# An encoder kernel whose weight, sum and working tiles start 32 bytes later in SBUF

## The chip, the cores and the metric

The kernel runs on one core of one Trainium2 chip. The metric is the device time of one execution in microseconds; several executions are made and their median is compared. SBUF is the on-chip memory of the core, 128 partitions deep; an address below is the byte offset within a partition, the same for all 128.

## The reference

The computation is a two-layer encoder over 256 tokens of width 1024, in float32. Per layer:

```
x = x + 0.5 * swiglu(rms_norm(x, ffn1_norm[l]), ffn1_w_gate[l], ffn1_w_up[l], ffn1_w_down[l])
h = rms_norm(x, mix_norm[l])
proj = h @ w_in[l]
qa, ka, va, qb, kb, vb = jnp.split(proj, SPLITS, axis=-1)
out_a = windowed_gqa_sink(qa, ka, va, sink[l], slopes_a)
out_b = differential_attention(qb, kb, vb, lam, slopes_b)
out_b = (rms_norm(out_b, diff_subln[l]) * (1.0 - lam_init)).reshape(b, s, B_V_COLS)
x = x + jnp.concatenate([out_a, out_b], axis=-1) @ w_out[l]
x = x + 0.5 * swiglu(rms_norm(x, ffn2_norm[l]), ffn2_w_gate[l], ffn2_w_up[l], ffn2_w_down[l])
```

and `swiglu(h, w_gate, w_up, w_down)` is `(silu(h @ w_gate) * (h @ w_up)) @ w_down` with a hidden width of 2816. A last RMS norm gives the output. Nearly all of the arithmetic is in the matrix products with the weights: four feed-forward blocks and two attention blocks.

## The kernel before

Every product with a weight is made with three matmuls. A weight arrives in SBUF as float32 in a raw tile (`emit_dma`, line 164; tag `raw`, 6 buffers of 8192 bytes per partition). `emit_split` (line 207) turns a raw tile into a high and a low part: ScalarE casts to float32r (`hi`), VectorE subtracts (`lo = raw - hi`). The parts lie in the pool `s4` (28 buffers of 4096 bytes), which also holds the activations, split in the same way. `tokens` (line 613) then issues, for each chunk of 128 of the contraction and each of the two blocks of 128 tokens, `xh*hi`, `xl*hi` and `xh*lo` into one PSUM bank. The activation is the stationary operand (128 x 128) and the weight the moving one (128 x 512 columns, 2048 bytes of each partition).

Within a feed-forward block the hidden width is walked in groups of 512 columns. In most groups `by_sevens` (line 745) replaces the eight products of a 2 x 2 block form by seven products of sums: `prod` (line 709) issues them, with sums of weights made in the raw tiles (by VectorE, or by a transfer that adds while it writes) and sums of activations made once per block by `make_sums` in working tiles with the tags `q` and `v` (line 401). In the attention block `narrow` (line 637) has the weight as the stationary operand and the activation as the moving one, 512 columns wide for `hi` and 256 for `lo`; `scores` (line 989) multiplies queries and keys on half of the rows, two at a time; products of probabilities and values use plain float32. Transposes go through TensorE, with the data as stationary operand and `ident` as moving one.

The order of the matmuls is the program's own (`pe` keeps it always, line 69), and the other engines keep the program's order in the feed-forward blocks. How early a weight is fetched and split is set by `ahead` (line 248) with the tuned numbers in `LEAD` (line 32). A scheduler places the instructions of the attention block by a model of their times.

Memory: four pools lie one behind the other, and each tile takes a multiple of 32 bytes.

```
const = ctx.enter_context(tc.tile_pool(name="const", bufs=1))
wp = ctx.enter_context(tc.tile_pool(name="wp", bufs=1))
s4 = ctx.enter_context(tc.tile_pool(name="s4", bufs=N_S4))
tp = ctx.enter_context(tc.tile_pool(name="tp", bufs=1))
```

The pool `const` holds the residual stream `xk`, the identity `ident`, small constants and the tables of distances; `wp` the raw weights; `s4` split weights and activations; `tp` working tiles. In the kernel before, the tiles lie here:

| tile (pool) | first address | beyond a multiple of 64 |
|---|---|---|
| xk (const) | 16512 | 0 |
| ident (const) | 25216 | 0 |
| wake (const) | 25728 | 0 |
| ones (const) | 26272 | 32 |
| distB, distA (const) | 27552, 29600 | 32 |
| gsub, lex (const, the last two) | 32096, 32128 | 32, 0 |
| raw (wp), 6 of 8192 bytes | 32160 | 32 |
| s and w (s4), 28 of 4096 bytes | 81312 | 32 |
| tmp (tp), 5 of 2048 bytes | 198304 | 32 |
| q (tp), 3 of 4096 bytes | 208544 | 32 |
| v (tp), 4096 bytes | 220832 | 32 |
| vA (tp), 1024 bytes | 226336 | 32 |

In the profile the tiles of `s4` are named `w` (split weights) and `s` (all else), and almost all instructions have the line of the helper that records them, so groups are told apart by their tiles and shapes. A row of the timeline merges neighbours of one kind.

Of the kernel before, what the change touches and what calls it, by code (L numbers as in the profile page):

```python
# [9 lines left out]
F32 = mybir.dt.float32  # L10
# [4 lines left out]
P = 128  # L15
# [31 lines left out]
def trunk(ctx: ExitStack, tc: tile.TileContext, x, n1, g1, u1, d1, nm, w_in, sink,  # L47
# [23 lines left out]
    const = ctx.enter_context(tc.tile_pool(name="const", bufs=1))  # L71
# [479 lines left out]
    lsum = const.tile([P, 2, DEPTH], F32, name="lsum")  # L551
    nlam = const.tile([P, DEPTH], F32, name="nlam")
    gsub = const.tile([P, DEPTH], F32, name="gsub")
    slopeA = [2.0 ** -(h + 1) for h in range(8)]
    slopeB = [2.0 ** -(2 * (h + 1)) for h in range(4)]
    lam_init = [0.8 - 0.6 * math.exp(-0.3 * l) for l in range(DEPTH)]
# [733 lines left out]
```

## Time and profile before

| what | value |
|---|---|
| time, three runs | 909.51, 909.10, 909.54 us; median 909.51 us |
| span of the profiled execution, first to last instruction | 907.5 us |
| median less that span | 2.0 us |
| mean granted clock of TensorE | 0.999 |
| TensorE busy | 899.1 us |
| VectorE busy | 785.9 us |
| ScalarE busy | 609.8 us |
| read from HBM | 199.0 MB, 220 GB/s over the span |

For the profiled execution only its span is recorded, not a time of its own; the times come from separate executions. Engines are named PE (TensorE's matmuls), PEld (its weight loads), DVE (VectorE), ACT (ScalarE), POOL (GpSimd) and SP (a queue for transfers). A row of a group gives its tiles as out<-in, its shape, its count, then busy microseconds, the mean nanoseconds of one, and the idle time of the engine before it with what ended it. A matmul's busy span reaches over the start of the next one, so how fast matmuls follow each other is read from starts.

### The profile page before, as it was taken

How to read it: one execution, taken by the hardware profiler on the slowest of the kernel's cores; microseconds unless marked ns; L12 is line 12 of the kernel's file. 1: busy time of each engine (PE TensorE's matmuls, PEld its weight loads, DVE VectorE, ACT ScalarE, POOL GpSimd, SP SyncE). 2: the span in 40 equal slices, each digit the busy share in tenths (PEclk: the TensorE clock that was granted, in tenths of full speed). 3: DMA queues.
4: the chain of work that ended last, by engine and by line, in shares of the span. 5: the costliest groups of instructions: out<-in, count | busy, mean ns of one | idle time of the engine just before them, and what ended most of it. 6: DMA issues, size and time to landing. Idle time of an engine off the chain costs nothing.

```text
span 907.5 us, 12030 instructions
## 1 busy us (share of the span) xinstructions
PE 899.1 (99%) x4468; PEld 751.0 (83%) x4468; DVE 785.9 (87%) x1069; ACT 609.8 (67%) x970; POOL 63.2 (7%) x79
## 2 busy tenths in 40 slices
PE   9999999999999999999999999999999999999997
PEld 7888888888888888888888888888888888888886
DVE  5968999879987899999778999988888978999894
ACT  6946677666776776677575776667667785776660
POOL 0401000000001001000000001000000000101011
PEclk9999999999999999999999999999999999999999
DMA  9998897954148798897976898899611786898731
GB/s 328 355 287 213 236 309 247 268 143 179 47 150 241 174 265 247 247 300 256 279 204 171 250 278 258 252 303 248 182 57 48 263 223 166 234 312 255 219 114 47
DMA packets 114331, 200.83 MB, mean 221 GB/s; under 512 B 3678, under 2 KB 31648, under 8 KB 114272
## 3 DMA queue, kind: packets, MB, share of 16 engines
q1 hardware_dynamic: 97616, 167.66, 54.4%
q0 software_dynamic: 16096, 31.75, 20.1%
q8 instruction: 35, 0.57, 0.2%
q10 hardware_dynamic: 560, 0.66, 0.2%
q14 instruction: 24, 0.20, 0.1%
HBM read 199.00 MB, written 1.05 MB: 220 GB/s over the span
## 4 chain that ended last, share of the span: by engine, by line
PE 98%; DMA 1%; issue 0%; SPq 0%; DVE 0%; POOLq 0%; POOL 0%
PE ps L62 73%; PE xy L62 25%; DMA xk<-in_x_dram 1%; SPq L172 0%; DVE s L62 0%; DVE xk L62 0%; POOLq L1285 0%; POOL rf L62 0%; SPq L469 0%; SPq L465 0%; DVE tot L62 0%; DVE tmp L62 0%
## 5 line engine op out<-in xcount | busy, mean ns | idle before, releaser
L62 DVE TENSOR_TENSOR w<-raw,w 128x1024 fp32r<-128x1024 f32 (+1 forms) x458 | 476.4, 1097 | 34.6 <-ACT w L62 33.2
L62 PE MATMUL ps<-w,s 128*128 128x512 f32 (+1 forms) x2046 | 473.6, 389 | 0.0
L62 PEld LDWEIGHTS ps<-w,s 128*128 128x128 f32 x2046 | 379.9, 188 | 78.7 <-issue 0.8
L62 ACT CAST w<-raw 128x1024 fp32r<-128x1024 f32 (+1 forms) x457 | 403.9, 954 | 54.0 <-DVE raw L62 38.7
L62 PE MATMUL xy<-w,s 128*128 128x512 f32 x528 | 125.8, 392 | 0.0
L62 PEld LDWEIGHTS xy<-w,s 128*128 128x128 f32 x528 | 98.2, 188 | 20.4
L62 PE MATMUL xy<-w,q 128*128 128x512 f32 x360 | 88.1, 393 | 0.0
L62 PEld LDWEIGHTS xy<-w,q 128*128 128x128 f32 x360 | 66.5, 188 | 13.3
L62 PE MATMUL ps<-s,w 128*128 128x512 f32 (+1 forms) x384 | 69.8, 338 | 0.0
L62 DVE TENSOR_TENSOR raw<-raw,raw 128x2048 f32<-128x2048 f32 x30 | 68.6, 2288 | 0.5
L62 POOL DMA_DIRECT2D raw<-in_ffn_w_up_dram x30 | 38.9, 1313 | 430.1 <-DVE w L62 264.9
L62 PEld LDWEIGHTS ps<-s,w 128*128 128x128 f32 x384 | 58.6, 188 | 8.5
L62 ACT ACTIVATE s<-ps,gcol 128x256 fp32r<-128x256 f32 (+1 forms) x80 | 31.4, 479 | 34.0 <-PE ps L62 34.0
L62 ACT CAST s<-ps 128x512 fp32r<-128x512 f32 x36 | 20.4, 592 | 43.2 <-PE ps L62 43.0
L62 PE MATMUL ps<-w,q 128*128 128x512 f32 x180 | 43.2, 389 | 0.0
L62 PE MATMUL ps<-w,v 128*128 128x512 f32 x180 | 43.2, 389 | 0.0
L62 DVE TENSOR_TENSOR s<-ps,s 128x512 fp32r<-128x512 f32 x36 | 24.1, 686 | 19.5 <-ACT s L62 19.3
L62 PEld LDWEIGHTS ps<-w,v 128*128 128x128 f32 x180 | 33.8, 188 | 7.0
L62 PEld LDWEIGHTS ps<-w,q 128*128 128x128 f32 x180 | 33.8, 188 | 7.0
L62 ACT ACTIVATE s<-s,negm 128x256 f32<-128x256 f32 x64 | 31.8, 498 | 5.3 <-DVE negm L62 5.3
L62 ACT COPY ps<-ps 128x512 f32<-128x512 f32 x15 | 8.6, 570 | 34.4 <-PE ps L62 34.4
L62 DVE SCALAR_TENSOR_TENSOR s<-ps,gcol,s 128x256 fp32r<-128x256 f32 x48 | 20.3, 477 | 13.0 <-ACT s L62 12.9
(131 smaller groups left out, 584.3 us busy)
## 6 DMA issues: line engine op xcount, KB each, us to landing
raw<-in_ffn_w_down_dram SPq DMA_DIRECT2D x44, 1024.0 KB, 7.0
raw<-in_ffn_w_gate_dram SPq DMA_DIRECT2D x39, 1024.0 KB, 7.7
raw<-in_ffn_w_up_dram SPq DMA_DIRECT2D x39, 1024.0 KB, 7.1
raw<-in_ffn_w_up_dram POOLq DMA_DIRECT2D x30, 1024.0 KB, 10.0
raw<-in_w_in_dram SPq DMA_DIRECT2D x14, 1024.0 KB, 6.7
raw<-in_ffn_w_gate_dram SPq DMA_DIRECT2D x8, 512.0 KB, 7.9
raw<-in_ffn_w_up_dram SPq DMA_DIRECT2D x8, 512.0 KB, 8.9
raw<-in_w_in_dram SPq DMA_DIRECT2D x8, 512.0 KB, 6.0
```

The lines of the kernel that those rows point to most:

```text
L62: ins = issue(*a, **k)
```

## The change

One tile is added at the end of the list of constants. No instruction writes or reads it.

```
     lsum = const.tile([P, 2, DEPTH], F32, name="lsum")
     nlam = const.tile([P, DEPTH], F32, name="nlam")
     gsub = const.tile([P, DEPTH], F32, name="gsub")
+    const.tile([P, 8], F32, name="edge")
     slopeA = [2.0 ** -(h + 1) for h in range(8)]
```

It takes 8 floats, 32 bytes of each partition, between `gsub` and `lex`. All that lies behind it starts 32 bytes later: `lex`, and the pools `wp`, `s4` and `tp` as wholes. The raw tiles then start at 32192, the tiles of `s4` at 81344, `tmp` at 198336, `q` at 208576, `v` at 220864 and `vA` at 226368, all multiples of 64. What lies in front of it, `xk`, `ident`, `wake`, `ones` and the tables of distances among it, stays. The instructions are the same.

More of the change, by code (lines that the diff above doesn't have):

```diff
@@ L553, in trunk @@
     gsub = const.tile([P, DEPTH], F32, name="gsub")
+    const.tile([P, 8], F32, name="edge")
     slopeA = [2.0 ** -(h + 1) for h in range(8)]
```

## The prediction

> **What bounds the kernel now.** The page of the profile comes first: the span, the engines' busy shares and the chain of work that ended last.
>
> ```profile
> span 907.5 us, 12030 instructions
> PE 899.1 (99%) x4468; PEld 751.0 (83%) x4468; DVE 785.9 (87%) x1069; ACT 609.8 (67%) x970; POOL 63.2 (7%) x79
> ...
> PEclk9999999999999999999999999999999999999999
> ...
> PE 98%; DMA 1%; issue 0%; SPq 0%; DVE 0%; POOLq 0%; POOL 0%
> ```
>
> TensorE carries 98% of the chain at a full granted clock. The view of waits of TensorE has two rows in the whole run:
>
> ```profile
> PE ps L62 <- DVE wake L62: 1.0, 1, 1.0
> PE ps L62 <- DMA xk<-in_x_dram: 0.7, 1, 0.7
> ```
>
> Both lie in the first microseconds, so after the start no transfer and no other engine holds TensorE up. The time is then the sum of the intervals at which matmuls follow each other. Busy time can't give these, because one matmul's busy span (389 ns) overlaps the next; starts in the timeline of TensorE can. First a stretch in the middle, then two stretches of the end, whose first rows start in the same run of 256-column matmuls, then attention.
>
> ```profile
> 305.36 1.04 PE L62 MATMUL ps<-ident,s 128*128 128x128 f32 x8
> 306.19 3.01 PE L62 MATMUL xy<-w,q 128*128 128x512 f32 x12
> 309.04 8.32 PE L62 MATMUL ps<-w,s 128*128 128x512 f32 x36
> 317.20 2.88 PE L62 MATMUL ps<-w,q 128*128 128x512 f32 x12
> ```
>
> ```profile
> 896.82 4.00 PE L62 MATMUL ps<-w,s 128*128 128x256 f32 x32
> ...
> 898.74 2.08 PE L62 MATMUL ps<-w,s 128*128 128x256 f32 x16
> ```
>
> ```profile
> 244.63 2.78 PE L62 MATMUL ps<-ident,s 128*128 128x128 f32 x24
> 247.25 3.74 PE L62 MATMUL xy<-v,s 128*128 128x128 f32 x32
> 250.82 1.91 PE L62 MATMUL ps<-ident,s 128*128 128x128 f32 x16
> ```
>
> From the start of one row to the start of the next, divided by the count: 512 columns take 8.16 us / 36 = 226.7 ns; 256 columns take (898.74 - 896.82) / 16 = 120.0 ns. The difference of 106.7 ns for 256 columns is 0.417 ns a column, and what is left is a constant: 226.7 - 512 x 0.417 = 13.3 ns per matmul, the same at both widths. That constant is the one thing in the bound that an address could touch.
>
> **The change, part by part.** It adds a tile of 8 floats, 32 bytes per partition, that nothing reads or writes. It removes no instruction, adds no wait and moves nothing past a queue. All raw weights, split weights, sums and working tiles go from 32 past a multiple of 64 to a multiple of 64; xk, ident and wake, in front of the new tile, stay at multiples of 64, and ones stays at 32 past. Since all moved tiles go together, which of them lie beside each other is unchanged. Four kinds of access remain.
>
> VectorE, ScalarE and their operands: no cost. xk lies at a multiple of 64 already, tmp does not, and the same operation takes the same time:
>
> ```profile
> L62 DVE TENSOR_TENSOR tmp<-xy,tmp 128x512 f32<-128x512 f32 x30 | 19.2, 680 | 0.0
> ...
> L62 DVE TENSOR_TENSOR xk<-xk,ps 128x512 f32<-128x512 f32 x17 | 11.2, 681 | 2.2 <-PE ps L62 2.2
> ```
>
> Weight loads: no cost either. A transpose loads its data as weights, from s (32 past) or from xk (a multiple), 140 against 142 ns:
>
> ```profile
> L62 PEld LDWEIGHTS ps<-ident,s 128*128 128x128 f32 x240 | 28.0, 140 | 3.8
> L62 PEld LDWEIGHTS ps<-ident,xk 128*128 128x128 f32 x96 | 11.4, 142 | 2.9 <-DMA xk<-in_x_dram 1.1
> ```
>
> Transfers into raw: no row shows their price by address. It is covered as long as TensorE waits for none of them; without that cover the first stretch below would show it.
>
> Moving operands of matmuls: this is the open price. Every fast matmul streams w, s or q, now 32 past a multiple; no row has the same form with a moving operand at a multiple. The groups by form give the counts:
>
> ```profile
> L62 PE MATMUL ps<-w,s 128*128 128x512 f32 x2010 | 469.3, 390 | 0.0
> L62 PE MATMUL xy<-w,s 128*128 128x512 f32 x528 | 125.8, 392 | 0.0
> L62 PE MATMUL xy<-w,q 128*128 128x512 f32 x360 | 88.1, 393 | 0.0
> L62 PE MATMUL ps<-s,w 128*128 128x512 f32 x192 | 68.2, 398 | 0.0
> L62 PE MATMUL ps<-s,w 128*128 128x256 f32 x192 | 53.5, 278 | 0.0
> L62 PE MATMUL ps<-w,q 128*128 128x512 f32 x180 | 43.2, 389 | 0.0
> L62 PE MATMUL ps<-w,v 128*128 128x512 f32 x180 | 43.2, 389 | 0.0
> L62 PE MATMUL xy<-s,w 128*128 128x512 f32 x32 | 11.5, 395 | 0.0
> L62 PE MATMUL ps<-s,q 64*128 64x256 f32 x144 | 10.7, 289 | 0.0
> L62 PE MATMUL xy<-s,w 128*128 128x256 f32 x32 | 8.9, 278 | 0.0
> L62 PE MATMUL ps<-w,s 128*128 128x256 f32 x36 | 4.5, 283 | 0.0
> L62 PE MATMUL xy<-s,q 64*128 64x256 f32 x48 | 3.5, 279 | 0.0
> ```
>
> That is 3482 of 512 columns, 260 of 256, and 192 on half the rows that run in pairs and count as 96: 3838 in all. Each could gain between nothing and its whole constant, 13.3 ns: 0 to 51 us. Below nothing is the third rival. Between the ends there is one pair of rows that differs in the moving operand's address at one width, though also in the kind of work: transposes stream ident (a multiple) at 2.62 us / 24 = 109.2 ns, products stream v (32 past) at 3.57 us / 32 = 111.6 ns. They say 2.4 ns, or 9 us over 3838. My own value comes from counting: a run of 2048 bytes that starts 32 past a multiple of 64 touches 33 units of 64 bytes and not 32, a run of 1024 bytes 17 and not 16, so both widths pay one unit, as the constant does. A unit is 16 columns, 16 x 0.417 = 6.7 ns. It lies in the middle of the bounds, and I take it: 3838 x 6.7 = 25.6 us.
>
> [...]
>
> What is late next? The windows of single stages say it (length, then PE, PEld, DVE, ACT and POOL busy, clock, share of the DMA engines, GB/s):
>
> ```profile
> 19.60:69.40 49.80, 49.80 (x229) 41.20 (x228) 38.56 (x47) 35.07 (x52) 12.52 (x31) 1.00 1.04 324
> ...
> 401.60:432.40 30.80, 30.80 (x142) 25.60 (x141) 29.65 (x28) 22.25 (x26) 0.00 (x0) 1.00 0.81 269
> ...
> 515.60:546.40 30.80, 30.80 (x141) 25.60 (x141) 29.50 (x28) 21.85 (x27) 2.57 (x2) 1.00 0.92 267
> ```
>
> In the first stretch the transfers are full (share 1.04), so a faster TensorE would meet late weights there, and its 229 x 6.7 = 1.5 us are lost. A stage of 30.80 us has some 132 fast matmuls; at 0.88 us less it is 29.92 us long, and VectorE is busy for up to 29.65 us of it. It still fits, with little room; I take off 1 us for stalls, an estimate from that room over the fifteen stages of this length. The sum is 25.6 - 1.5 - 1.0 = 23 us. Against the profiled span it is 907.5 - 23 = 884.5 us; the median, 909.5 us, lies 2.0 us above that span (launch and end, untouched), so the forecast is **886.5 us**. If each matmul gave its whole 13.3 ns, a stage would want 29.04 us of TensorE and be held at 29.65 us by VectorE in the fullest; with 3 us lost in the first stretch, 4 us in the full stages and some 3 us of stalls (estimates from these windows), 51 - 10 = 41 us would be left: 868 us. By the pair of ident and v it is 909.5 - 9 = 900 us. The forecast's own range is 868 to 901 us.
>
> **The rivals.** First, nothing happens: **909.5 us**. The constant may belong to this kind of matmul, and the address may not matter. For it: 13.3 ns is twice one unit of 64 bytes, so my count leaves half unexplained, and units of 128 bytes explain all of it: 226.7 / 0.417 = 544 columns is 17 units of 32 columns, and 120.0 / 0.417 = 288 is 9 units, just what a run that starts off a multiple of 128 touches. The new addresses are 64 past a multiple of 128 and would still touch 17 and 9. Against it: the pair of ident and v. Here belongs also that the change doesn't do what it says, if an unused tile took no room; the small tiles each take room of their own in the layout of before, so I give that little.
>
> [...]
>
> Second, TensorE gains and another bound takes most of it: VectorE has 29.65 of 30.80 us in the fullest stages, and works in order behind ScalarE's casts. Were its work stretched by waits to the whole stage, only the parts outside the fifteen stages, 907.5 - 15 x 30.8 = 445 us or half, would gain: 909.5 - 12 = 898 us. This lies inside the forecast's range and shares its chance.
>
> Third, on the other side: the new start is the worse one. The 12 matmuls behind the 8 transposes at 305.36 us take 309.04 - 305.36 - 8 x 0.109 = 2.81 us, 234 ns each and not 226.7, though no wait is shown: weight loads and moving runs have phases in which they disturb each other for a dozen matmuls until they settle. If runs that begin at multiples of 64 keep weight load and moving run in such a phase, each pays 7.3 ns: 3838 x 7.3 = 28 us, **937 us**. It decides from some 250 matmuls that don't settle (1.8 us, 0.2%). For it: the phase exists. Against it: it dies out at every place, and weight loads show no price by address.
>
> **How the numbers follow.** The measurement tells about 0.2% from no change, 907.7 to 911.3 us. Forecast with its range of prices 0.50; nothing 0.37; worse start 0.13. The range goes from the forecast's lower end to the nothing case: 868 to 911 us, which leaves the third rival out. Faster 0.50, same 0.37, slower 0.13.
>
> **What would show it.** In the timeline the 36 matmuls that now take 8.16 us: 7.92 us (220 ns each) by the forecast, 7.68 us with the whole constant gone, 8.16 us if nothing happens, 8.4 us by the third rival. The 256-column matmuls at the end must lose the same ns each as the wide ones, and the transposes must keep 109.2 ns; the products with v should lose 2.4 ns if their price was one of address. TensorE's waits stay near 1.7 us in all but for the first stretch. The prediction is wrong if intervals stay and the time changes, or if they fall and waits for VectorE or raw eat the gain.

## The result, and the profile after

| | before | after |
|---|---|---|
| time, median of 21 runs | 909.34 us | 910.51 us |
| lowest and highest | 908.75, 911.16 us | 910.12, 911.39 us |
| span of the profiled execution | 907.5 us | 909.3 us |

The ratio is 1.0013, with a 95% interval of 1.0007 to 1.0019: 1.2 us slower, and not 23 us faster. The page of the changed kernel looks like that of before:

```profile
span 909.3 us, 12030 instructions
PE 900.7 (99%) x4468; PEld 752.0 (83%) x4468; DVE 787.0 (87%) x1069; ACT 610.2 (67%) x970; POOL 62.1 (7%) x79
...
PE 98%; DMA 1%; issue 0%; SPq 0%; DVE 0%; POOLq 0%; POOL 0%
```

TensorE is still the chain, at 98%. The timeline of TensorE of the changed kernel, at the place that the prediction named, and then the products with v:

```profile
310.40 8.32 PE L62 MATMUL ps<-w,s 128*128 128x512 f32 x36
318.56 2.88 PE L62 MATMUL ps<-w,q 128*128 128x512 f32 x12
```

```profile
248.56 3.74 PE L62 MATMUL xy<-v,s 128*128 128x128 f32 x32
252.13 1.91 PE L62 MATMUL ps<-ident,s 128*128 128x128 f32 x16
```

36 matmuls take 318.56 - 310.40 = 8.16 us, as before: 226.7 ns each at the new addresses. The products with v take 3.57 us / 32 = 111.6 ns, also as before, though v now starts at a multiple of 64.

Where do 1.2 us come from, then? Both kernels issue the same 4468 matmuls in the same order, so the starts can be compared one by one. Past the first microseconds they drift apart almost only in two places per layer, both in `narrow`, the products of the attention block in which a matmul of 512 columns (`hi`) and one of 256 (`lo`) take turns. The timeline of before, in layer 0:

```profile
187.98 1.04 PE L62 MATMUL ps<-ident,xk 128*128 128x128 f32 x8
188.77 1.64 PE L62 MATMUL ps<-s,w 128*128 128x512 f32 x8
...
197.18 0.40 PE L62 MATMUL ps<-tmp,ones 128*128 128x256 f32 x2
197.42 16.80 PE L62 MATMUL ps<-s,w 128*128 128x512 f32 x96
214.15 0.98 PE L62 MATMUL ps<-s,q 64*128 64x256 f32 x12
```

and of the changed kernel:

```profile
188.81 1.04 PE L62 MATMUL ps<-ident,xk 128*128 128x128 f32 x8
189.61 1.66 PE L62 MATMUL ps<-s,w 128*128 128x512 f32 x8
...
198.17 0.39 PE L62 MATMUL ps<-tmp,ones 128*128 128x256 f32 x2
198.40 17.12 PE L62 MATMUL ps<-s,w 128*128 128x512 f32 x96
215.45 0.98 PE L62 MATMUL ps<-s,q 64*128 64x256 f32 x12
```

The first stretch of 24 pairs goes from 197.18 - 188.77 = 8.41 us to 198.17 - 189.61 = 8.56 us, the second of 48 pairs from 214.15 - 197.42 = 16.73 us to 17.05 us: 0.15 and 0.32 us. Layer 1 repeats it; in the chain of before and of the changed kernel its second stretch, with a few matmuls beside it, stands as

```profile
643.20 17.78 PE ps L62 x110
```

```profile
644.62 18.10 PE ps L62 x110
```

Together this is 2 x (0.15 + 0.32) = 0.94 us, inside the interval of the measured difference. (The two spans lie 1.8 us apart because of another 0.7 us in the first 9 us of this one profile; in a second profile of the changed kernel, below, these are less than 0.1 us.)

Inside a stretch the starts settle into a pattern. Before, a pair takes 350 and 343 ns by turns, 346.7 ns on average, which is 226.7 + 120.0. After, it takes 361, 349 and 350 ns by turns, 353.3 ns. (A row's length divided by its pairs is somewhat more, since the last interval runs up to the next row.) There are 112 pairs per layer: stretches of 8, 24, 48, 16 and 16. Before, the stretches of 24 and 48 settle at 346.7 ns and the others near 353.5 ns; after, all of them are at the slow pattern. 72 pairs x 6.67 ns x 2 layers = 0.96 us.

### The profile page after: what moved, and what is told of

It is laid out like the page before. It is cut to its first block, busy times and chain, and to the rows that moved or that the text cites. A ratio compares the mean times of both kernels' runs of the same rounds, so it can differ in the third digit from the quotient of the medians.

```text
span 909.3 us, 12030 instructions
## 1 busy us (share of the span) xinstructions
PE 900.7 (99%) x4468; PEld 752.0 (83%) x4468; DVE 787.0 (87%) x1069; ACT 610.2 (67%) x970; POOL 62.1 (7%) x79
## 4 chain that ended last, share of the span: by engine, by line
PE 98%; DMA 1%; issue 0%; SPq 0%; DVE 0%; POOLq 0%; POOL 0%
PE ps L62 73%; PE xy L62 25%; DMA xk<-in_x_dram 1%; SPq L172 0%; DVE s L62 0%; DVE xk L62 0%; POOLq L1286 0%; POOL rf L62 0%; SPq L469 0%; SPq L465 0%; DVE tot L62 0%; DVE tmp L62 0%
## 5 line engine op out<-in xcount | busy, mean ns | idle before, releaser
L62 PE MATMUL ps<-ident,s 128*128 128x128 f32 x240 | 31.4, 272 | 0.0
```

Source lines behind the costliest of these rows:

```text
L62: ins = issue(*a, **k)
```

## The experiments

The question is what sets this pattern, and whether the constant of 13.3 ns per matmul, on which the forecast was built, can be touched by any address. Ratios are to the kernel before, with 95% intervals where a kernel was timed several times. The patterns of all ten stretches are read from the starts of matmuls in each profile.

**The two kernels once more, and two other shifts.** again_before and again_after repeat the kernels for a second profile. pad64 and pad96 only change the size of the unused tile:

```
+    const.tile([P, 16], F32, name="edge")     # pad64
+    const.tile([P, 24], F32, name="edge")     # pad96
```

again_before:

> The kernel before once more, for its profile. Address theory (the start address decides at which interval the pairs of 512 and 256 columns in narrow settle): the same 72 of 112 pairs per layer at about 346.7 ns and the other 40 at about 353.5 ns as in its first profile. Entry theory (chance phases at the entry of each stretch decide, whatever the address): stretches may settle otherwise than in the first profile. Both: 512-column matmuls of tokens and prod at 226.7 ns.

again_after:

> The changed kernel once more, for its profile. Address theory: all 112 pairs per layer at about 353.3 ns again. Entry theory: some stretches at 346.7 ns this time. The 0.8 us lost in the first 6 us of its first profile should be gone if it was chance.

pad64:

> The unused tile is 64 bytes: raw, s, w, tmp, q and v lie 64 bytes later than before, 32 past a multiple of 64 again. Address theory by 64: as before, 1.000 of its time, 72 pairs per layer at 346.7 ns. If what counts is 128 (96 past a multiple now, 32 before): could be either. Entry theory: time anywhere between 0.999 and 1.0015, no relation to the address.

pad96:

> The unused tile is 96 bytes: all moved tiles at multiples of 128 (and s and w of 256). Theory that the constant of 13.3 ns per matmul comes from touching one more unit of 128 bytes: 512-column matmuls at 213 to 220 ns, 0.95 to 0.97 of the time before. Theory that the constant belongs to the form of the matmul: 226.7 ns. Then, by the address theory by 64, narrow as in the changed kernel, all pairs at 353.3 ns and about 1.0013.

again_before took 909.39 us and again_after 910.35 us, one run each, with spans of 907.6 and 908.5 us. All ten stretches settled as in the first profile of the same kernel, and again_after doesn't lose the time at the start. So the pattern is a property of the kernel, not of the run. pad64 came out at 1.0001 (0.9992 to 1.001), with the last 16 pairs of each layer fast as well (88 of 112 pairs), and pad96 at 1.0001 (0.9992 to 1.001). In the timeline of pad96, whose s and w start at multiples of 256:

```profile
308.91 8.32 PE L62 MATMUL ps<-w,s 128*128 128x512 f32 x36
317.07 2.88 PE L62 MATMUL ps<-w,q 128*128 128x512 f32 x12
```

Again 8.16 us for 36. A run of 2048 bytes touches 16 units of 128 bytes here and 17 in the kernel before, and the interval is 226.7 ns in both: neither units of 64 nor of 128 bytes carry the constant. pad96 is at a multiple of 64 like the changed kernel and yet narrow is as fast as before in its layer 0, so the remainder by 64 doesn't set the pattern there either. Its layers differ, though:

```profile
197.22 16.81 PE L62 MATMUL ps<-s,w 128*128 128x512 f32 x96
213.96 0.98 PE L62 MATMUL ps<-s,q 64*128 64x256 f32 x12
...
643.15 17.11 PE L62 MATMUL ps<-s,w 128*128 128x512 f32 x96
660.19 0.98 PE L62 MATMUL ps<-s,q 64*128 64x256 f32 x12
```

The rows are of layer 0 (16.74 us) and of layer 1 (17.04 us).

**Is narrow the whole price?** two_by_two reorders narrow at the old addresses, and two_by_two_32 does the same at the changed ones:

```
-        for i, (wk, xk) in enumerate(kcs):
-            wh, wl = w.part(wk, h=j)
-            xv = xs[xk // 2][:, xk % 2]
-            pe.matmul(acc, lhsT=wh, rhs=xv, start=first and i == 0, stop=False)
-            pe.matmul(acc[:, S:512], lhsT=wl, rhs=xv[:, 0:S], start=False, stop=last and i == len(kcs) - 1)
+        for i in range(0, len(kcs), 2):
+            two = [(w.part(wk, h=j), xs[xk // 2][:, xk % 2]) for wk, xk in kcs[i:i + 2]]
+            for n, ((wh, wl), xv) in enumerate(two):
+                pe.matmul(acc, lhsT=wh, rhs=xv, start=first and i + n == 0, stop=False)
+            for n, ((wh, wl), xv) in enumerate(two):
+                pe.matmul(acc[:, S:512], lhsT=wl, rhs=xv[:, 0:S], start=False, stop=last and i + n == len(kcs) - 1)
```

two_by_two:

> Addresses as before; narrow issues two matmuls of 512 columns, then the two of 256, and not in turns. Theory that the 1.2 us of the change are pairs in narrow settling at 353.3 ns and not at 346.7 ns: with two short ones in a row the weight load has another place, all stretches of narrow should settle at 346.7 ns a pair or below, 80 slow pairs of 6.7 ns gone, about 0.5 us less, 0.9994. Theory that narrow is as fast as it can be in the fast stretches only by chance: no change, or all pairs at 353.3 ns, 1.001.

two_by_two_32:

> The same order of matmuls with the changed addresses. If the whole price of the change lies in how the pairs of narrow settle, this one takes the same time as two_by_two, within 0.0005 of it. If the addresses cost time elsewhere, it stays about 0.001 above two_by_two.

They took 0.9999 (0.999 to 1.0008) and 1.0002 (0.9993 to 1.0011). In both, all ten stretches settle at 697 ns for four matmuls, 348.3 ns a pair: 16.81 us for 48 pairs at the old addresses and, in the timeline of two_by_two_32, at the changed ones:

```profile
198.00 16.89 PE L62 MATMUL ps<-s,w 128*128 128x512 f32 x96
214.82 0.98 PE L62 MATMUL ps<-s,q 64*128 64x256 f32 x12
```

With another order the difference between the addresses is gone within the stretches. The hoped-for 0.5 us isn't there, since the new pattern lies 1.7 ns a pair above the fast one. The medians, 909.19 and 909.41 us, can't be told apart.

**Which tiles?** s4tp_32 puts the 32 bytes behind the raw tiles, tp_32 in front of the working tiles alone:

```
+    wp.tile([P, 8], F32, name="edge")     # s4tp_32, in the changed kernel's place
+    tp.tile([P, 8], F32, name="edge")     # tp_32, ahead of all other tiles of tp
```

s4tp_32:

> The unused tile of 32 bytes lies between the raw tiles and the pool s4: raw as before, s, w and all working tiles at multiples of 64. If the price hangs on the addresses of the operands of narrow: as the changed kernel, 1.0013, all pairs at 353.3 ns. If it hangs on where transfers write: 1.000.

tp_32:

> The unused tile lies at the front of the pool tp: raw, s and w as before, working tiles (tmp, q, v) alone at multiples of 64. Narrow reads s and w only. If the price hangs on the addresses of its operands: 1.000 of the time before and the pattern of before (72 of 112 pairs per layer at 346.7 ns). If it hangs on the working tiles: 1.0013.

s4tp_32 came out at 1.001 (1.0001 to 1.0019), with all pairs at the slow pattern as in the changed kernel, so where transfers write the raw tiles has no part in it. tp_32 was the surprise: 914.25 us, 1.0056 (1.0042 to 1.007), four times the price of the change itself. Its timeline:

```profile
372.32 8.33 PE L62 MATMUL ps<-w,s 128*128 128x512 f32 x36
380.49 2.96 PE L62 MATMUL ps<-w,q 128*128 128x512 f32 x12
383.29 2.96 PE L62 MATMUL xy<-w,q 128*128 128x512 f32 x12
386.09 2.96 PE L62 MATMUL ps<-w,v 128*128 128x512 f32 x12
388.89 11.05 PE L62 MATMUL ps<-w,s 128*128 128x512 f32 x48
```

beside the same place of before:

```profile
370.68 8.32 PE L62 MATMUL ps<-w,s 128*128 128x512 f32 x36
378.84 2.88 PE L62 MATMUL ps<-w,q 128*128 128x512 f32 x12
381.56 2.88 PE L62 MATMUL xy<-w,q 128*128 128x512 f32 x12
384.28 2.88 PE L62 MATMUL ps<-w,v 128*128 128x512 f32 x12
```

Matmuls of w and s stay at 226.7 ns. Those whose stationary operand is a sum (q, v), now moved against the moving w, go from 2.72 us to 2.80 us a dozen, 226.7 to 233.3 ns, with no wait shown. There are 720 of them; by their starts they take 4.3 us more in all, and the spans differ by 4.9 us. The sums lie here at the changed kernel's addresses (q at 208576) and w at those of before (81312 on), and in each of those two kernels the interval is 226.7 ns. So it is how the two operands' addresses stand to each other that goes with 226.7 or 233.3 ns here, and not where either stands on its own.

Narrow missed its expectation, too. It reads s and w only, which lie as before, and so do ident and xk; yet its stretches, 0.4 us slower in all, don't keep the pattern of before:

```profile
189.53 1.64 PE L62 MATMUL ps<-s,w 128*128 128x512 f32 x8
...
197.94 0.40 PE L62 MATMUL ps<-tmp,ones 128*128 128x256 f32 x2
198.17 17.11 PE L62 MATMUL ps<-s,w 128*128 128x512 f32 x96
215.21 0.98 PE L62 MATMUL ps<-s,q 64*128 64x256 f32 x12
```

The 24 pairs take 8.41 us, as before, but the 48 pairs 17.04 us, as in the changed kernel, and layer 1 does the same. The 24 follow transposes of xk with ident, which both stayed. The 48 follow two matmuls that read ones, which stayed, and tmp, which moved. The last 16 pairs, behind transposes of tmp, are now fast. So the pattern of a stretch can change with none of its own operands moved, when a tile moves that the matmuls just ahead read. (tp_64, below, agrees: its stretches of 8 and 24 pairs are as before; the 48 are slow and the first of the two stretches of 16 is fast, behind matmuls that read tmp and q.)

**Everything moved together.** all_32 puts the 32 bytes ahead of all tiles, and ident_32 between xk and ident:

```
+    const.tile([P, 8], F32, name="edge")     # all_32: ahead of xk
+    const.tile([P, 8], F32, name="edge")     # ident_32: behind xk and grow1, ahead of ident
```

all_32:

> The unused tile of 32 bytes lies in front of all tiles: every tile moves by 32, xk and ident too, and no tile moves against another. Theory that narrow settles by the absolute start (0 past 64: slow): as the changed kernel, all pairs at 353.3 ns, 1.001. Theory that what counts is how the addresses of one matmul's operands, and of the transposes just ahead (ident, xk), stand to each other: pattern of before, 72 of 112 pairs at 346.7 ns, 1.000.

ident_32:

> The unused tile lies between xk and ident: xk stays, ident and all behind it move by 32. So s and w stand to ident as before and to xk as in the changed kernel. If the relation to ident (moving operand of the transposes ahead) decides: the pattern of before, 72 of 112 pairs per layer at 346.7 ns, 1.000. If the relation to xk (their stationary operand) decides: all pairs at 353.3 ns, 1.001.

all_32 took 0.9999 (0.999 to 1.0008). Its s, w, raw and sums have exactly the changed kernel's addresses, but ident and xk have moved too, and the pattern of before is back in all ten stretches. ident_32 took 1.0 (0.9991 to 1.0009): only xk and grow1 (read once, at the start) stay behind, and the stretches of 24 and 48 pairs are fast in both layers. In its timeline:

```profile
188.11 1.03 PE L62 MATMUL ps<-ident,xk 128*128 128x128 f32 x8
188.90 1.64 PE L62 MATMUL ps<-s,w 128*128 128x512 f32 x8
...
197.31 0.40 PE L62 MATMUL ps<-tmp,ones 128*128 128x256 f32 x2
197.54 16.80 PE L62 MATMUL ps<-s,w 128*128 128x512 f32 x96
214.28 0.98 PE L62 MATMUL ps<-s,q 64*128 64x256 f32 x12
```

8.41 and 16.74 us, as before. So it isn't the relation to xk. What moved with s and w here and not in the changed kernel is ident and the constants behind it; of these, the transposes just ahead of the 24 pairs stream ident, and the two matmuls just ahead of the 48 pairs read ones.

**Which relations are good, and is there a better one?** tp_64 puts 64 bytes in front of the working tiles. sum_8, sum_16 and sum_24 start each sum so many bytes into a tile 32 bytes longer, and step_128 makes the tiles 128 bytes longer:

```
-                sm = tp.tile([P, 2, 512], F32R, tag=tag, bufs=n, name=nm_(tag)).rearrange("p a (c s) -> p (a c) s", c=2)
+                sm = tp.tile([P, 1032], F32R, tag=tag, bufs=n, name=nm_(tag))[:, 2:1026].rearrange("p (a s) -> p a s", s=256)
```

(sum_8; 4:1028 in sum_16, 6:1030 in sum_24, and width 1056 with 0:1024 in step_128. In all four, the other two tiles with the tags q and v, the queries of `scores` and `vB`, get the same size and start at 0.)

tp_64:

> The unused tile at the front of tp is 64 bytes: the sums q and v (stationary) stand 64 bytes further from the split weights w (moving), at the same remainder by 64. Theory that stationary and moving operand disturb each other when their remainders by 64 differ: 226.7 ns for all matmuls of w and q or v, 1.000. Theory that it goes by 128 or more: 230 ns and above, as with 32 bytes, up to 1.0056.

sum_8:

> Each sum starts 8 bytes into its tile, and these tiles are 32 bytes longer: half of the matmuls of w and a sum have a stationary operand 8 bytes past the remainder of the moving one, half 40 bytes. Theory of remainders by 64: both halves above 226.7 ns, 231 to 235 ns, about 1.005 to 1.006. Theory of 32-byte halves of a unit: the half with 8 bytes stays at 226.7 ns, the other is at 233 ns, 1.003. Theory that the equal remainder is what costs the constant of 13.3 ns: the half with 8 bytes falls below 226.7 ns.

sum_16:

> The same with 16 bytes: half of the matmuls of w and a sum with 16 bytes between the remainders, half with 48. Theory of remainders by 64: both above 226.7 ns, 1.005 to 1.006. Theory of 32-byte halves: 16 bytes at 226.7 ns, 48 bytes at 233 ns, 1.003. Theory that the constant comes from the equal remainder: below 226.7 ns.

step_128:

> The sum tiles are 128 bytes longer, so that the three q buffers stand 256, 384 and 0 bytes (by 512) from the split weights and v 128. Theory that 0 and 256 are the good relations: the matmuls with those two q buffers at 226.7 ns, those with the third q and with v at 231 to 234 ns, some 2 to 3 us more. Theory that any multiple of 128 is good: 226.7 ns everywhere, the time of before. If a relation exists without the constant of 13.3 ns: one group below 226 ns.

sum_24:

> Sums start 24 bytes into tiles that are 32 bytes longer: q stands 280, 312 or 344 bytes (by 512) from the split weights, v 376. Theory that relations up to 16 bytes past 256 are good and those from 32 on are not: 280 in between or at 226.7 ns, 312 to 376 at 233 ns, some 3.5 to 4 us more. Theory that each group settles by chance: groups of one relation would mix 226.7 and 233 ns in stretches, in no order.

tp_64 took 1.0058 (1.0043 to 1.0073), sum_8 1.0039 (1.0025 to 1.0052) and sum_16 1.0044 (1.0031 to 1.0058); step_128 took 912.48 us and sum_24 912.25 us, one run each, beside 909.58 us of before. Since the longer tiles lie behind each other, the shifts add up from buffer to buffer, and the four buffers have four relations and not the two that the expectations of sum_8 and sum_16 counted. The table gives the mean interval of matmuls inside prod, by the distance of the stationary operand (of the next matmul, which is loaded meanwhile: in the kernel before the first load of a row of w and s starts at 308.82 us, between the matmuls that start at 308.81 and at 309.04 us) from the moving one, modulo 512 bytes. It is worked out from the starts in each trace and the tiles' addresses, for matmuls with at least 14 others of 512 columns ahead; which matmuls at the edges of a dozen are counted moves a mean by up to some 0.3 ns.

| distance, bytes | interval, ns | kernel, operand |
|---|---|---|
| 0 | 226.7 | before, s; step_128, q |
| 256 | 226.7 | before, q and v |
| 256 | 228.8 | step_128, q |
| 264, 272, 280 | 230.8, 226.7, 230.8 | sum_8, sum_16, sum_24, q |
| 288 | 233.1, 233.5 | tp_32, q, v |
| 296 | 228.4 | sum_8, q |
| 304, 312 | 233.3, 233.3 | sum_16, sum_24, q |
| 320 | 233.4, 233.6 | tp_64, q, v |
| 328, 336, 344 | 233.2, 231.9, 233.3 | sum_8, sum_16, sum_24, q |
| 360, 368, 376 | 233.3, 233.3, 226.8 | sum_8, sum_16, sum_24, v |
| 384 | 232.9 | step_128, q |
| 128 | 233.0 | step_128, v |

The equal remainder by 64 isn't enough: 64 bytes more (320) is as bad as 32. Distances 0 and 256 are good in the kernel before, most others cost 6.6 ns, and one far from both (376) costs nothing. No theory of sum_8, sum_16 or sum_24 fits: 8 and 24 bytes beyond 256 cost 4 ns, 16 bytes nothing. step_128 came out near the first of its theories: 2.9 us more, with the third q and v at 233 ns.

Two rows are means of unlike intervals. The 228.8 ns at 256 in step_128 come from the entry: behind a dozen at distance 384, the first seven intervals are 236, 224, 231, 236, 228, 233 and 230 ns, and the rest are at 226.7 ns. At 296 in sum_8, whole dozens differ. The middle row of each of these two places is one:

```profile
77.04 2.96 PE L62 MATMUL ps<-w,q 128*128 128x512 f32 x12
79.83 2.96 PE L62 MATMUL xy<-w,q 128*128 128x512 f32 x12
82.63 2.96 PE L62 MATMUL ps<-w,v 128*128 128x512 f32 x12
```

```profile
309.46 8.36 PE L62 MATMUL ps<-w,s 128*128 128x512 f32 x36
317.66 2.88 PE L62 MATMUL ps<-w,q 128*128 128x512 f32 x12
320.38 2.94 PE L62 MATMUL xy<-w,q 128*128 128x512 f32 x12
```

The dozen at 317.66 us takes 2.72 us, and so do all eight that follow matmuls of w and s: 226.7 ns from the first on. The dozen at 79.83 us takes 2.80 us; the three that follow a sum at distance 328 and the four that follow transposes stay near 233 ns to their end. So the distance of a matmul's own two operands doesn't decide alone: as in narrow, what ran just ahead has a part. No distance brought a mean below 226.7 ns.

**The odd kernel once more.**

> The kernel with 96 bytes once more, for its profile. In its first one the two long stretches of narrow settled at 346.7 ns in layer 0 and at 353.3 ns in layer 1, with the same instructions and relations in both. Theory that addresses alone decide: the same picture again. Theory that addresses only set how likely each interval is: another picture.

again_pad96 took 909.43 us and settled as in its first profile, layer by layer: fast in layer 0, slow in layer 1. So this isn't chance, but the relations followed here are the same in both layers and don't explain it. The buffers that hold s and w differ between the layers, by multiples of 4096 bytes; whether that matters wasn't tried.

## Why the prediction was wrong

**What bounds the kernel** was right: TensorE's intervals alone, with no wait on another engine past the start (1.1 and 0.9 us there in the changed kernel); every difference found, a fifth of the change's 1.2 us aside, is a difference of intervals. By the forecast's own sign, intervals that stay where it looked while the time changes, it was wrong.

**The step that failed** is the price of moving operands: "a run of 2048 bytes that starts 32 past a multiple of 64 touches 33 units of 64 bytes and not 32", 6.7 ns for each of 3838 matmuls. That each unit of 64 bytes costs time was the author's estimate, and no run shows it. The measured price is nothing: 226.7 ns at starts 32 past a multiple of 64, at multiples of 64 and at multiples of 128. The count explained only half of the constant; that misfit was noted and not given its due. With this term the losses taken off it fell too, since TensorE wasn't faster anywhere. That the measured 910.51 us lies inside the stated range, 868 to 911 us, is luck: the range ends at the nothing case, and no term of the sum has a part in it.

**The pair of ident and v** (109.2 against 111.6 ns) was read as a sign of an address. v moved to a multiple of 64, and its products kept 111.6 ns, so the 2.4 ns don't come from the start of v against a multiple of 64. The two rows differ in the kind of work, too; no run separates that.

**The first rival**, no change at 909.5 us, came nearest: 1.0 us below the measured 910.51 us. Its reason in units of 128 bytes was as wrong as the forecast's units of 64 (pad96). Its other reason, that the constant may belong to this kind of matmul and the address may not matter, holds in part: the constant of 13.3 ns fell at no address and at no distance, and the matmuls of w and s keep 226.7 ns at the old and at the new addresses; but in tp_32 the 720 matmuls of w and a sum settle at 233.3 ns.

**The third rival** came near in kind: intervals that grow with no wait shown, and in tp_32 by how the stationary operand stands to the moving one. That weight loads and moving runs disturb each other was the author's reading of that; the runs show the intervals and not their cause. Its size was nearly right, too (7.3 ns; measured 6.67 ns a pair in narrow), by luck: the starts show that most of the extra time of its dozen (69 of some 90 ns) lies in the step from the last transpose to the first matmul, and from the eighth on the intervals are 226.7 ns. It had the wrong trigger, the absolute start, and so the wrong reach: 144 pairs paid, not 3838 matmuls. The argument against it, that weight loads show no price by address, looked at how long a weight load takes (140 and 142 ns); the price doesn't show there, only in when the next matmul starts. In tp_32, too, the weight loads of w and a sum take 188 ns, as before.

**One sentence hid the cause**: "Since all moved tiles go together, which of them lie beside each other is unchanged." That holds for the moved tiles among each other, and prod therefore kept its time. It doesn't hold for ident and ones, which stayed and which the matmuls just ahead of narrow's two long stretches read. And the forecast counted q among the streamed tiles; in its rows the sums q and v are the stationary operands of the wide matmuls, and tp_32 shows that their place has a price, though only against that of the streamed w.

**What is shown, and what isn't.** Shown: 0.94 us of the change's 1.2 us are narrow's stretches in a slower pattern; the pattern repeats from profile to profile; moving all tiles, or all but xk and grow1, undoes it; with another order in narrow the stretches are equally long at both addresses; moving the working tiles alone, which narrow doesn't read, changes the pattern of stretches behind matmuls that read them (tp_32, tp_64). Argued: that in the change the tiles are ident for the 24 pairs and ones for the 48, and that a stretch locks into its pattern at its entry. Open: by which property of the addresses the intervals go, whether the reads of two operands meet in SBUF, and why pad96 differs from layer to layer. Stretches that settle at 346.7 ns in both layers throughout would save another 80 pairs x 6.67 ns = 0.5 us; no such kernel was found, and 0.06% is below what these runs tell apart.

## What to carry to other kernels

In this kernel, with TensorE busy for 99% of the span, padding a tile changed the time without changing an instruction, by 1.2 us in the change and 5.0 us in tp_32, and the effect went by how a matmul's stationary and moving operands stand to each other and by what the matmuls just ahead read; a pool shifted alone cost 0.56% here, all tiles moved together nothing (all_32, 0.9999). So before a small difference is put down to an edit that also moves tiles, compare the addresses and the intervals between starts of the same matmuls. And a constant in the time of an operation is no proof of a cause whose size happens to be half of it.

## What the runs showed of the hardware that had not been expected

Matmuls with the same shapes and no wait followed each other at mean intervals from 226.7 to 233.6 ns, depending on the distance between their stationary and moving operands in SBUF and, at one distance (296 bytes in sum_8), on what ran just ahead; the busy time of one showed it too (mean 389 ns for ps<-w,v before, 396 ns in tp_32, whose row is this):

```profile
L62 PE MATMUL ps<-w,v 128*128 128x512 f32 x180 | 44.4, 396 | 0.0
```

In narrow, a stretch of alternating widths had several stable patterns (350 and 343 ns by turns, an even 346 to 347 ns in pad64 and pad96, 361, 349 and 350 ns by turns), kept the one it settled into over 48 pairs, and took the same one in both profiles of each of the three kernels that were profiled twice. In tp_32 its pattern changed though only tiles that the matmuls ahead of it read had moved.
